# A decoder step's prompt heads and cache rounds: older heads first, query copies on VectorE, a later second gather, and a gate in two parts

## The chip, the cores and the metric

The kernel runs on one core of one Trainium2 chip. The time is the device time of one execution in microseconds (us). The engines of the core are named as in the profile: PE is TensorE with its weight load PEld, DVE is VectorE, ACT is ScalarE, POOL is GpSimd, SP is SyncE, which here only starts DMAs.

## The reference

One inference step of a decoder trunk of two layers, with 256 prompt tokens and 8 samples of 8 tokens each (320 tokens in all). Each layer adds to x the merged output of three branches, each with a sigmoid gate:

```
xn = RMSNorm(x);  (h_pool, ..., h_gate) = split(xn @ w_in)
y_a = pool_mixer(h_pool) * silu(z_pool)
y_b = MLA(h_q, h_kv, h_kr, cache) * silu(z_mla)     # 8 heads, 64 nope + 32 rope, latent 256
y_c = gated_delta(h_qkv, ...) * silu(z_dn)
gates = sigmoid(h_gate)                             # 3 x 1024 columns
x = x + (g0*(y_a@w_br_pool) + g1*(y_b@w_br_mla) + g2*(y_c@w_br_dn)) @ w_out
```

The change lies in the attention of MLA and in the gates that are computed beside it. The prompt attends causally to itself; a sample attends to the 2048 cached tokens of its own 16 pages, which a page table names, and to its own 8 new tokens. Softmax is over both together.

## The kernel before

Every projection is a float32 matmul done as three products: `split_w` makes of a weight block its rounded high part wh (ACT, L196) and the rest wl (a subtraction, L197, on DVE, or on POOL where the call says `spare`), and `mm3` (L209 to 222) sums wh times the high part of xn, wh times its low part, and wl times its high part. A gate is one block of 128 of the 3072 gate columns: `gate_w` loads and splits its weight, `gate_mm` issues 24 matmuls of 128x320 (8 blocks of k, three products each), `gate_out` multiplies by the norm's factor on DVE (L460), takes tanh on ACT (L461) and, if the gate is to be spilled, starts its store from ACT's queue (L464). Gates are spread over the attention, so that PE has work where the attention's chain leaves it without.

From L1332 on the order on PE, DVE, ACT and POOL is the order in which the program is written (a manual schedule); each engine works through its instructions in that order, and waits where an operand isn't ready. There are two parts.

**The heads** (L1349 and on, h from 0 to 10) are the prompt's attention, a pipeline over 8 heads. A step h copies the query of head h into one of two buffers qx (`head_query`: two copies, nope and rope, L1260 and L1261, on POOL), computes its scores (psc on PE, L1272), adds the causal mask while it leaves PSUM (pS on DVE, L1274), takes the two negated maxima (L1276, L1277) and the two exponentials (ACT, L1278 and L1279). Then it scales head h-1 (reciprocal on DVE L1283, 128 columns on ACT L1284, 256 columns on POOL L1285), transposes the P of head h-2 (pT on PE, L1290, copied by ACT, L1292), and multiplies head h-3's P with the values (po, L1299 and L1300), which DVE puts into zs (L1301). `gather(bb)` starts two indirect DMAs on POOL's queue, kv (2 MB, L1133) and kr (256 KB, L1134), for the pages of sample bb; gather 0 stands ahead of the heads, gather 1 behind head 0's scores. Two gates (steps `GP`) lie in the heads, and five DVE transposes (`flip`, L1153 and L1150) turn sample 0's gathered keys into KT and krT in steps 4 to 8.

**The rounds** (L1376 and on, bb from 0 to 7) are the samples' attention to the cache. A round scales the scores sc (L1163) into S with a running maximum (`soften`, L1185), joins it with the maximum over the sample's own tokens (mo) and across the two halves of the partitions (`swap`, L1180: two copies of 64 partitions), takes exp (L1195 to L1197), transposes P (PT on PE, L1212, copied by ACT in two parts, L1213; PTn for the own tokens, L1221), multiplies it with kv (pv, 33 matmuls, L1235 and L1239), scales the result (o, L1241) and computes the next round's sc. Beside it run one or two gates (GL), and the DVE transposes of the next sample's keys, five a round. `weigh` (L1199) makes the factor 1/sum for o. Three kv buffers and two kr buffers hold the gathers; q is loaded by four DMAs of SP's queue (L1140), the gate weights by others of it into four buffers.

Of the kernel before, what the change touches and what calls it, by code (L numbers as in the profile page):

```python
# [11 lines left out]
F32 = mybir.dt.float32  # L12
# [30 lines left out]

GP, GL, SPILL = (0, 4), (2, 2, 2, 2, 2, 2, 1, 1), 14

# [71 lines left out]
def trunk(tc, I, O, layers=2):  # L117
# [90 lines left out]

    def mm3(out, w, x, nk, first=0):  # L209
        wh, wl = w  # L210
        xh, xl = x
        if l == 0 and turn[0] <= WLP:
            for k in range(nk):
                nc.tensor.matmul(out, wh[:, k, :], xh[:, first + k, :], start=k == 0, stop=False)
                nc.tensor.matmul(out, wh[:, k, :], xl[:, first + k, :], start=False, stop=False)
            for k in range(nk):
                nc.tensor.matmul(out, wl[:, k, :], xh[:, first + k, :], start=False, stop=k == nk - 1)
            return
        for k in range(nk):
            nc.tensor.matmul(out, wh[:, k, :], xh[:, first + k, :], start=k == 0, stop=False)  # L220
            nc.tensor.matmul(out, wh[:, k, :], xl[:, first + k, :], start=False, stop=False)  # L221
            nc.tensor.matmul(out, wl[:, k, :], xh[:, first + k, :], start=False, stop=k == nk - 1)  # L222
# [187 lines left out]
    for l in range(layers):  # L410
# [40 lines left out]

        def gate_mm(tag, w):
            b = ps(tag, "gate")
            mm3(b[:, :T], w, xn, 8)
            return b
# [429 lines left out]
        so = p2.tile([128, 4, 64], F32, name="so")  # L885
        mo = p2.tile([128, 4], F32, name="mo")
        cko = p2.tile([64, 256], F32, name="cko")
# [72 lines left out]
        def latent_queries():  # L960
# [22 lines left out]
            for j in range(4):  # L983
# [4 lines left out]
                stt(so[:, j], sc[:, :64], SCALE, c("win")[:, 48 - 16 * j : 112 - 16 * j], mult, add)  # L988
            nc.vector.tensor_reduce(mo, so, AX.X, amax)

# [178 lines left out]
        def stats(bb):  # L1169
            mx = pa.tile([128, 12], F32, tag="mx", name="mx", bufs=2)  # L1170
            nc.gpsimd.memset(mx, 0.0)
            nc.gpsimd.memset(mx[:, 2:3], NEG)
            own, j = halves[bb % 2], bb // 2
            nc.gpsimd.tensor_copy(mx[own, 2:3], mo[own, j : j + 1])
            return mx

        def swap(eng, mx, k):

            for er, other in (halves, halves[::-1]):
                eng.tensor_copy(mx[er, 11:12], mx[other, k : k + 1])  # L1180

        def soften(bb, sc, mx):
# [5 lines left out]
            )  # L1188
            tt(mx[:, 3:4], mx[:, 1:2], mx[:, 2:3], amax)  # L1189
            swap(nc.gpsimd, mx, 3)  # L1190
            return S
# [6 lines left out]

        def weigh(mx):  # L1199

            tt(mx[:, 9:10], mx[:, 5:6], mx[:, 6:7], add)
            swap(nc.vector, mx, 9)
            tt(mx[:, 10:11], mx[:, 9:10], mx[:, 11:12], add)
            nc.vector.reciprocal(mx[:, 10:11], mx[:, 10:11])
# [52 lines left out]
        def head_query(h):  # L1257
            p, er = eight[h]
            e, rr = h % 2, slice(32 * (h % 4), 32 * (h % 4) + 32)
            nc.gpsimd.tensor_copy(qx[e][er], qn[er, p, :TP])  # L1260
            nc.gpsimd.tensor_copy(qx[e][rot[e]], qr[rr, h // 4, :TP])  # L1261

# [19 lines left out]
        def head_scale(S, st2):  # L1282
            nc.vector.reciprocal(st2[:, 4:6], st2[:, 2:4])  # L1283
            act(S[:, :128], S[:, :128], AF.Copy, scale=st2[:, 4:5])  # L1284
            nc.gpsimd.tensor_scalar(S[:, 128:], S[:, 128:], st2[:, 5:6], None, mult)  # L1285
# [45 lines left out]
        with tc.manual_schedule(engines={mybir.EngineType.PE, mybir.EngineType.DVE, mybir.EngineType.Activation, mybir.EngineType.Pool}):  # L1331
# [6 lines left out]
            q4 = load_q(0)  # L1338
            nm, w = gate_w()
            for t in range(2):  # L1340
# [8 lines left out]
            for h in range(11):  # L1349
                if h < 8:  # L1350
                    head_query(h)
                    hs[h] = head_scores(h)
                if h == 0:
                    gather(1)
                if h - 1 in hs:
                    head_scale(*hs[h - 1])
                if h - 2 in hs:
                    hp[h - 2] = head_turned(hs[h - 2][0])
                if h - 3 in hs:
                    head_attend(h - 3, hp[h - 3])  # L1360
                if h in GP:
                    b = gate_mm("A", w)
                    gate_out(nm, b, True)
                    if h == GP[-1]:
                        pair[0] = paired[0] = 1
                    nm, w = gate_w() if h < GP[-1] else (None, None)
                if 4 <= h < 9:
                    flip(0, keys, parts_[h - 4])
            phc.close()
# [6 lines left out]
            for bb in range(NB):  # L1376
                more = bb + 1 < NB
                S = soften(bb, sc, mx)
                if bb + 2 < NB:
                    gather(bb + 2)  # L1380
                if more:
# [11 lines left out]
                if more:  # L1393
                    flip(bb + 1, keys, 4)
                    flip(bb + 1, keys, 2)
                for nm, w in gs[1:]:
                    b = gate_mm("A", w)
                    gate_out(nm, b, bb < 6)
                weigh(mx)
                PT = turned_p(S)  # L1400
                PTn = turned_own(bb)
                o = attend(bb, PT, PTn, mx)
                if more:
# [118 lines left out]
```

## Time and profile before

| | |
|---|---|
| Median of 3 runs | 1108.27 us (1102.31 to 1115.26) |
| The profiled execution | 1106.15 us, span 1104.4 us |
| Mean granted clock of PE in it | 0.952 |
| Busy | PE 90%, DVE 64%, ACT 42%, POOL 30% |
| Heads of layer 0 (first psc to first sc) | 289.27 to 341.41 us |
| Heads of layer 1 | 827.08 to 877.31 us |
| One round with two gates | 18.1 us |

Busy shares are means over the span, in which the projections with a nearly full PE take most of the time. What the heads and the rounds wait for is read in their own stretches. A clock of 1.00 is PE's upper level of 2.4 GHz, 0.50 the lower of 1.2 GHz. In the timelines, "xN" joins N like instructions, and the bracket at a row's end gives the idle time of that engine before it and what ended that.

### The profile page before, as it was taken

Reading aid. Unit: us, or ns where it says so; the run is one execution under the profiler, and the core shown is the slowest. Engines: PE = TensorE matmul, PEld = TensorE weight load, DVE = VectorE, ACT = ScalarE, POOL = GpSimd, SP = SyncE. Lnnn points to the kernel's source line nnn. Section 1 sums busy time; section 2 is a strip of 40 time slices with the busy share of each in tenths; the row PEclk is TensorE's granted clock in tenths of the full one; section 3 lists DMA queues with packets and bytes.
Section 4 is the critical chain, followed back from the end, with each engine's and each line's share of the span. In section 5 each row is a group of like instructions: output and inputs, shape, how many; then the busy total and the mean of one; then the engine's idle time right before and its main releaser. Section 6 shows DMA issues by size and latency. Waiting matters only on the chain.

```text
span 1104.4 us, 24792 instructions
## 1 busy us (share of the span) xinstructions
PE 996.2 (90%) x10179; PEld 867.7 (79%) x10179; DVE 709.0 (64%) x1341; ACT 460.7 (42%) x826; POOL 336.4 (30%) x527
## 2 busy tenths in 40 slices
PE   8988999999668999989988978999994799999996
PEld 7867898988456878779978867899783577777996
DVE  3999875656336656548748988656752665554872
ACT  5563253633323333244545534345242333333553
POOL 3655221232232111016355542211432211110531
PEclk8999899999868999999999989999996899999998
DMA  8523333625704666348763332364274186741961
GB/s 223 167 77 99 93 102 104 177 76 135 243 21 147 205 237 199 114 132 232 179 192 96 90 87 75 104 175 111 83 211 127 37 260 187 258 149 55 271 189 48
DMA packets 202698, 159.22 MB, mean 144 GB/s; under 512 B 27704, under 2 KB 191826, under 8 KB 200010
## 3 DMA queue, kind: packets, MB, share of 16 engines
q1 hardware_dynamic: 176364, 98.47, 32.8%
q0 software_dynamic: 7424, 48.75, 12.4%
q10 hardware_dynamic: 18798, 10.44, 3.3%
q8 instruction: 80, 1.31, 0.5%
q14 instruction: 32, 0.26, 0.1%
HBM read 144.17 MB, written 13.68 MB: 143 GB/s over the span
## 4 chain that ended last, share of the span: by engine, by line
PE 48%; DMA 15%; DVE 14%; issue 13%; ACT 6%; POOL 4%; ACTq 0%; SPq 0%; POOLq 0%; DVEq 0%
DMA kr<-in_cache_k_rope,idr 12%; PE pj L220 5%; PE pj L222 4%; PE pj L221 4%; DVE cy L505 4%; PE br L220 3%; PE br L221 3%; PE br L222 2%; DVE wl L197 2%; PE wo L220 2%; PE wo L221 2%; PE wo L222 2%; PE psc L1272 2%; PE gate L222 2%; PE gate L220 2%
## 5 line engine op out<-in xcount | busy, mean ns | idle before, releaser
L197 DVE TENSOR_TENSOR wl<-wraw,wh 128x1024 fp32r<-128x1024 f32 (+2 forms) x169 | 195.8, 1167 | 107.3 <-ACT wh L196 106.4
L196 ACT ACTIVATE wh<-wraw 128x1024 fp32r<-128x1024 f32 (+1 forms) x180 | 166.2, 935 | 177.3 <-PE pj L221 90.5
L220 PE MATMUL pj<-xnH,wh 128*128 128x320 f32 (+1 forms) x528 | 173.1, 328 | 16.7 <-DVE V L497 8.9
L222 PE MATMUL pj<-xnH,wl 128*128 128x320 f32 (+1 forms) x528 | 170.4, 323 | 6.7 <-DVE wl L197 6.3
L221 PE MATMUL pj<-xnL,wh 128*128 128x320 f32 (+1 forms) x528 | 168.2, 319 | 0.0
L220 PE MATMUL gate<-xnH,wh 128*128 128x320 f32 x384 | 123.9, 323 | 1.5 <-DVE V L497 1.5
L222 PE MATMUL gate<-xnH,wl 128*128 128x320 f32 x384 | 120.7, 314 | 1.6 <-DVE wl L197 1.3
L220 PEld LDWEIGHTS pj<-xnH,wh 128*128 128x128 f32 (+1 forms) x528 | 101.6, 192 | 24.7 <-ACT wh L196 6.9
L221 PE MATMUL gate<-xnL,wh 128*128 128x320 f32 x384 | 119.6, 312 | 0.0
L222 PEld LDWEIGHTS pj<-xnH,wl 128*128 128x128 f32 (+1 forms) x528 | 101.6, 193 | 11.8 <-DVE wl L197 8.1
L221 PEld LDWEIGHTS pj<-xnL,wh 128*128 128x128 f32 (+1 forms) x528 | 101.7, 193 | 3.2 <-issue 1.8
L220 PEld LDWEIGHTS gate<-xnH,wh 128*128 128x128 f32 x384 | 73.1, 190 | 9.2 <-issue 6.9
L1153 DVE STREAM_TRANSPOSE KT<-kv 128x1024 f32<-128x1024 f32 x64 | 78.5, 1226 | 0.1
L222 PEld LDWEIGHTS gate<-xnH,wl 128*128 128x128 f32 x384 | 73.0, 190 | 3.1 <-DVE wl L197 1.8
L221 PEld LDWEIGHTS gate<-xnL,wh 128*128 128x128 f32 x384 | 73.1, 190 | 1.1 <-issue 0.8
L1235 PE MATMUL pv<-kv,PT 128*64 128x256 f32 x512 | 58.8, 382 | 15.0 <-ACT PT L1213 15.0
L220 PE MATMUL br<-yH,wh 128*128 128x320 f32 x192 | 60.4, 318 | 4.2 <-ACT wh L196 2.2
L1235 PEld LDWEIGHTS pv<-kv,PT 128*64 128x64 f32 x512 | 35.4, 137 | 33.3 <-ACT PT L1213 17.2
L221 PE MATMUL br<-yL,wh 128*128 128x320 f32 x192 | 59.8, 313 | 0.0
L1163 PE MATMUL sc<-KT,q 32*64 32x256 f32 x2048 | 59.3, 377 | 0.0
L222 PE MATMUL br<-yH,wl 128*128 128x320 f32 x192 | 59.3, 312 | 0.0
L1180 POOL COPY mx<-mx 64x1 f32<-64x1 f32 x32 | 5.7, 179 | 167.6 <-DVE mx L1189 166.7
(408 smaller groups left out, 2108.8 us busy)
## 6 DMA issues: line engine op xcount, KB each, us to landing
wraw<-in_w_in SPq DMA_DIRECT2D x114, 512.0 KB
wraw<-in_w_out SPq DMA_DIRECT2D x16, 512.0 KB
q<-q4d SPq DMA_DIRECT2D x64, 72.0 KB
gate<-gt ACTq DMA_DIRECT2D x28, 160.0 KB
gt<-gate POOLq DMA_DIRECT2D x28, 160.0 KB, 3.6
wraw<-in_w_br_pool SPq DMA_DIRECT2D x16, 256.0 KB
wraw<-in_w_br_dn SPq DMA_DIRECT2D x16, 256.0 KB
wraw<-in_w_br_mla SPq DMA_DIRECT2D x16, 256.0 KB
```

The lines of the kernel that those rows point to most:

```text
L196: act(h, raw, AF.Copy)
L197: (nc.gpsimd.tensor_tensor if spare or turn[0] in K["lo"] else tt)(lo, raw, h.bitcast(F32), sub)
L220: nc.tensor.matmul(out, wh[:, k, :], xh[:, first + k, :], start=k == 0, stop=False)
L221: nc.tensor.matmul(out, wh[:, k, :], xl[:, first + k, :], start=False, stop=False)
L222: nc.tensor.matmul(out, wl[:, k, :], xh[:, first + k, :], start=False, stop=k == nk - 1)
L505: stt(y, V[:, j : j + 344], wj(j), y, mult, add)
L1153: nc.vector.transpose(v[:, a], kv[:, a * 1024 : a * 1024 + 1024].rearrange("p (i k c) -> p i k c", i=4, k=8))
L1163: nc.tensor.matmul(sc[64 * hf : 64 * hf + 64, g, :256], q4[r, k, :], krT[r, keys_] if k == 8 else KT[r, k, keys_], start=k == 0, stop=k == 8,)
L1180: eng.tensor_copy(mx[er, 11:12], mx[other, k : k + 1])
L1235: nc.tensor.matmul(pv[64 * hf : 64 * hf + 64, :256], PT[:, n * 128 + 64 * hf : n * 128 + 64 * hf + 64], kv[:, r : r + 256], start=n == 0, ...
L1272: nc.tensor.matmul(o, qx[e][kr, tq], kn[e][kr, p, :nk], start=True, stop=True)
```

## The change

In the heads: a step now scales head h-1 before it computes head h's scores; the query copies are DVE's (L1262, L1263) and stand one head ahead (head 0's ahead of the values, head h+1's in step h); the scale of the 128 columns goes from ACT to POOL (L1286, beside the 256 columns, L1287); the weights of both gates have their wl on POOL; the gates move from steps 0 and 4 to steps 1 and 5, their matmuls ahead of `head_attend`, the rest behind it; gather 1 moves from step 0 to step 3; DVE's transposes of the keys move from steps 4 to 8 to steps 3 to 7.

In the rounds: the first swap is DVE's; mo is kept in a form with the other half at a very low value, so that the copy and memset of `stats` go (its one reduction becomes two of 64 partitions, with one memset for a layer); the sum in `weigh` is POOL's, and gather bb+2 stands behind it instead of behind `soften`; in rounds with two gates the second gate's matmuls are issued in two parts of 12, P's transposes between them, and `gate_out`, `weigh` and pv behind the second part.

```diff
-GP, GL, SPILL = (0, 4), (2, 2, 2, 2, 2, 2, 1, 1), 14
+GP, GL, SPILL = (1, 5), (2, 2, 2, 2, 2, 2, 1, 1), 14
...
-        def gate_mm(tag, w):
-            b = ps(tag, "gate")
-            mm3(b[:, :T], w, xn, 8)
+        def gate_mm(tag, w, b=None, ks=(0, 8)):
+            b = b or ps(tag, "gate")
+            mm3(b[:, :T], w, xn, 8, ks=ks)
             return b
...
-        mo = p2.tile([128, 4], F32, name="mo")
+        mo = p2.tile([128, 4, 2], F32, name="mo")
+        nc.gpsimd.memset(mo, NEG)
...
-            nc.vector.tensor_reduce(mo, so, AX.X, amax)
+
+            for e, er in enumerate(halves):
+                nc.vector.tensor_reduce(mo[er, :, e], so[er], AX.X, amax)
...
             nc.gpsimd.memset(mx, 0.0)
-            nc.gpsimd.memset(mx[:, 2:3], NEG)
-            own, j = halves[bb % 2], bb // 2
-            nc.gpsimd.tensor_copy(mx[own, 2:3], mo[own, j : j + 1])
             return mx
...
-            tt(mx[:, 3:4], mx[:, 1:2], mx[:, 2:3], amax)
-            swap(nc.gpsimd, mx, 3)
+            tt(mx[:, 3:4], mx[:, 1:2], mo[:, bb // 2, bb % 2 : bb % 2 + 1], amax)
+            swap(mx, 3)
...
-        def weigh(mx):
-
-            tt(mx[:, 9:10], mx[:, 5:6], mx[:, 6:7], add)
-            swap(nc.vector, mx, 9)
+        def weigh(bb, mx):
+
+            nc.gpsimd.tensor_tensor(mx[:, 9:10], mx[:, 5:6], mx[:, 6:7], add)
+            if bb + 2 < NB:
+                gather(bb + 2)
+            swap(mx, 9)
...
-            nc.gpsimd.tensor_copy(qx[e][er], qn[er, p, :TP])
-            nc.gpsimd.tensor_copy(qx[e][rot[e]], qr[rr, h // 4, :TP])
+            nc.vector.tensor_copy(qx[e][er], qn[er, p, :TP])
+            nc.vector.tensor_copy(qx[e][rot[e]], qr[rr, h // 4, :TP])
...
-            act(S[:, :128], S[:, :128], AF.Copy, scale=st2[:, 4:5])
+            nc.gpsimd.tensor_scalar(S[:, :128], S[:, :128], st2[:, 4:5], None, mult)
...
-            nm, w = gate_w()
+            nm, w = gate_w(True)
+            head_query(0)
...
             for h in range(11):
-                if h < 8:
-                    head_query(h)
-                    hs[h] = head_scores(h)
-                if h == 0:
-                    gather(1)
                 if h - 1 in hs:
                     head_scale(*hs[h - 1])
+                if h < 7:
+                    head_query(h + 1)
+                if h == 3:
+                    gather(1)
+                if h < 8:
+                    hs[h] = head_scores(h)
                 if h - 2 in hs:
                     hp[h - 2] = head_turned(hs[h - 2][0])
+                if h in GP:
+                    b = gate_mm("A", w)
                 if h - 3 in hs:
                     head_attend(h - 3, hp[h - 3])
                 if h in GP:
-                    b = gate_mm("A", w)
                     gate_out(nm, b, True)
                     if h == GP[-1]:
                         pair[0] = paired[0] = 1
-                    nm, w = gate_w() if h < GP[-1] else (None, None)
-                if 4 <= h < 9:
-                    flip(0, keys, parts_[h - 4])
+                    else:
+                        nm, w = gate_w(True)
+                if 3 <= h < 8:
+                    flip(0, keys, parts_[h - 3])
...
                 S = soften(bb, sc, mx)
-                if bb + 2 < NB:
-                    gather(bb + 2)
...
-                for nm, w in gs[1:]:
-                    b = gate_mm("A", w)
-                    gate_out(nm, b, bb < 6)
-                weigh(mx)
+                two = len(gs) > 1
+                if two:
+                    b = gate_mm("A", gs[1][1], ks=(0, 4))
                 PT = turned_p(S)
                 PTn = turned_own(bb)
+                if two:
+                    gate_mm("A", gs[1][1], b, (4, 8))
+                    gate_out(gs[1][0], b, bb < 6)
+                weigh(bb, mx)
                 o = attend(bb, PT, PTn, mx)
```

The order of the instructions at three places follows. In brackets stand the counters for which an instruction waits; those with DMASW count the transfers of POOL's queue, given in turn, and at this place kv and kr of gather 0 have DMASW5 and DMASW6, those of gather 1 DMASW7 and DMASW0.

POOL at the start of layer 0's heads, before:

```order
L1134 DMA kr<-in_cache_k_rope,idr_2158 128x512 [waits DMASW6_49,DMASW0_49]
L1260 COPY qx_3356<-qn 64x256 [waits DMASW4_49,DMASW3_49]
L1261 COPY qx_3356<-qr 32x256 [waits Pool_49]
L1133 DMA kv<-in_cache_kv_latent,idr_2158 128x4096 [waits DMAHW2_49,DMAHW0_49,DMAHW4_49,DMASW7_49,PE_49]
L1134 DMA kr<-in_cache_k_rope,idr_2158 128x512
L1260 COPY qx_3357<-qn 64x256 [waits DMASW6_49,DMASW7_49,DMASW5_49,DMASW0_49]
L1261 COPY qx_3357<-qr 32x256 [waits Pool_49]
L1285 TENSOR_SCALAR pS<-pS,st_3391 128x256 [waits DVE_49,DMASW2_49,Activation_49,Pool_49]
```

and in the changed kernel:

```order
L1137 DMA kr<-in_cache_k_rope,idr_2158 128x512 [waits DMASW6_49,DMASW0_49]
L197 TENSOR_TENSOR wl<-wraw,wh 128x1024 [waits DMAHW2_49]
L1286 TENSOR_SCALAR pS<-pS,st_3395 128x128 [waits DMASW3_49,DMASW2_49,DVE_49]
L1287 TENSOR_SCALAR pS<-pS,st_3395 128x256 [waits Activation_49]
L197 TENSOR_TENSOR wl<-wraw,wh 128x1024 [waits DMAHW4_49,PE_49,Activation_49]
L1286 TENSOR_SCALAR pS<-pS,st_3410 128x128 [waits DVE_49]
L1287 TENSOR_SCALAR pS<-pS,st_3410 128x256
L1286 TENSOR_SCALAR pS<-pS,st_3460 128x128 [waits DVE_49]
L1287 TENSOR_SCALAR pS<-pS,st_3460 128x256 [waits Activation_49]
L1136 DMA kv<-in_cache_kv_latent,idr_2158 128x4096 [waits DMAHW0_49,DMASW7_49]
```

The copies are gone, the wl of the second head gate stands between the scales of heads 0 and 1, and the second gather behind those of head 2. Of the waits for POOL's own transfers, the first copy's stood for older ones, the second copy's for both gathers.

PE in the heads of layer 0 behind the values, before (psc of heads 0 to 2, the gate's first and last matmul):

```order
L1343 MATMUL vv<-wuv,hkv 128x512 x4
L1272 MATMUL psc<-kn,qx_3356 128x128
L1272 MATMUL psc<-kn,qx_3356 128x256
L220 MATMUL gate<-xnH,wh 128x320
...
L222 MATMUL gate<-xnH,wl 128x320
L1272 MATMUL psc<-kn,qx_3357 128x128
L1272 MATMUL psc<-kn,qx_3357 128x256
L1272 MATMUL psc<-kn,qx_3356 128x128
L1272 MATMUL psc<-kn,qx_3356 128x256
L1290 MATMUL pT<-cst,pS 128x128 x3
```

and in the changed kernel:

```order
L1274 MATMUL psc<-kn,qx_3358 128x128
L1274 MATMUL psc<-kn,qx_3358 128x256
L1274 MATMUL psc<-kn,qx_3359 128x128
L1274 MATMUL psc<-kn,qx_3359 128x256
L220 MATMUL gate<-xnH,wh 128x320
...
L222 MATMUL gate<-xnH,wl 128x320
L1274 MATMUL psc<-kn,qx_3358 128x128
L1274 MATMUL psc<-kn,qx_3358 128x256
L1292 MATMUL pT<-cst,pS 128x128 x3
L1274 MATMUL psc<-kn,qx_3359 128x128
L1274 MATMUL psc<-kn,qx_3359 128x256
L1292 MATMUL pT<-cst,pS 128x128 x3
```

The gate is now behind the scores of heads 0 and 1, and head 0's transposes ahead of head 3's scores.

PE in layer 0's first round, from the second gate's last matmuls on, before:

```order
L220 MATMUL gate<-xnH,wh 128x320
L221 MATMUL gate<-xnL,wh 128x320
L222 MATMUL gate<-xnH,wl 128x320
L1212 MATMUL PT<-cst,S 128x128 x8
L1221 MATMUL PTn<-cst,so 64x64
L1235 MATMUL pv<-kv,PT 64x256 x16
```

and in the changed kernel:

```order
L222 MATMUL gate<-xnH,wl 128x320
L1214 MATMUL PT<-cst,S 128x128 x8
L1223 MATMUL PTn<-cst,so 64x64
L220 MATMUL gate<-xnH,wh 128x320
...
L222 MATMUL gate<-xnH,wl 128x320
L1237 MATMUL pv<-kv,PT 64x256 x16
```

Between PTn and pv stand now 12 matmuls of the gate.

## Rows read from the trace of the kernel before

**Rows 1.** The page's parts 1 and 2: busy time, and granted clock in 40 slices.

```profile
PE 996.2 (90%) x10179; PEld 867.7 (79%) x10179; DVE 709.0 (64%) x1341; ACT 460.7 (42%) x826; POOL 336.4 (30%) x527
...
PEclk8999899999868999999999989999996899999998
```

**Rows 2.** Timeline of PE, heads: start us, us, engine, line, operation, tiles, [idle before].

```profile
289.27 0.82 PE L1272 MATMUL psc<-kn,qx 96*128 96x128 f32 x4
...
327.89 1.65 PE L1272 MATMUL psc<-kn,qx 96*128 96x128 f32 x4 [3.00 <-POOL qx L1261]
...
331.02 0.63 PE L1300 MATMUL po<-pPT,vv 128*64 128x128 f32 x2
...
341.41 3.71 PE L1163 MATMUL sc<-KT,q 32*64 32x256 f32 x128
...
827.08 0.82 PE L1272 MATMUL psc<-kn,qx 96*128 96x128 f32 x4
...
877.31 3.06 PE L1163 MATMUL sc<-KT,q 32*64 32x256 f32 x103
```

**Rows 3.** Waits of PE, heads of layers 0 and 1: us in total, times, longest.

```profile
PE psc L1272 <- POOL qx L1261: 18.1, 6, 6.6
...
PE psc L1272 <- POOL qx L1261: 20.0, 6, 7.6
```

**Rows 4.** Windows: us, busy time (and count) by engine, PEclk, DMA share, GB/s.

```profile
281.00:299.00 18.00, 12.62 (x66) 9.37 (x63) 3.81 (x8) 5.67 (x15) 4.65 (x5) 0.88 1.00 348
299.00:318.00 19.00, 10.57 (x31) 6.94 (x32) 6.46 (x18) 5.79 (x19) 5.82 (x11) 0.50 0.15 42
```

**Rows 5.** Chain of waits, 278 to 400: start us, us, what.

```profile
287.56 11.68 DMA kr<-in_cache_k_rope,idr
299.29 0.40 POOL qx L1260
...
366.96 10.48 DMA kr<-in_cache_k_rope,idr
```

**Rows 6.** Timeline of DVE, heads and rounds of layer 0.

```profile
324.72 0.52 DVE L1274 SCALAR_TENSOR_TENSOR pS<-psc,cst 128x384 f32<-128x384 f32 x1
...
326.19 1.23 DVE L1153 STREAM_TRANSPOSE KT<-kv 128x1024 f32<-128x1024 f32 x1
...
371.50 0.31 DVE L1180 COPY mx<-mx 64x1 f32<-64x1 f32 x2
...
382.89 1.24 DVE L1153 STREAM_TRANSPOSE KT<-kv 128x1024 f32<-128x1024 f32 x1
```

**Rows 7.** Waits of PE, rounds of layer 0 (341 to 466).

```profile
PE pv L1235 <- ACT PT L1213: 6.6, 7, 1.0
```

**Rows 8.** Timeline of PE, rounds with two gates and with one.

```profile
367.12 0.39 PE L220 MATMUL gate<-xnH,wh 128*128 128x320 f32 x1
...
370.71 1.04 PE L1212 MATMUL PT<-cst,S 128*128 128x128 f32 x8
...
372.96 3.67 PE L1235 MATMUL pv<-kv,PT 128*64 128x256 f32 x32 [1.04 <-ACT PT L1213]
...
459.59 3.67 PE L1235 MATMUL pv<-kv,PT 128*64 128x256 f32 x32 [0.42 <-ACT PT L1213]
```

**Rows 9.** Timeline of ACT, first gate in the heads (ACTq: its queue's DMA).

```profile
294.18 0.47 ACT L461 ACTIVATE gt<-gt 128x320 f32<-128x320 f32 x1 [2.10 <-DVE gt L460]
299.10 0.35 ACTq L464 DMA_DIRECT2D gate<-gt  x1
299.50 1.06 ACT L196 ACTIVATE wh<-wraw 128x1024 fp32r<-128x1024 f32 x1 [4.85 <-DMA q<-q4d]
```

**Rows 10.** Groups by line: busy us, mean ns of one, idle before.

```profile
L197 POOL TENSOR_TENSOR wl<-wraw,wh 128x1024 fp32r<-128x1024 f32 x11 | 26.6, 2415 | 14.5 <-ACT wh L196 14.4
```

**Rows 11.** Timeline of POOL, heads of layer 0.

```profile
282.58 1.33 POOL L1261 COPY qx<-qr 32x256 f32<-32x256 f32 x1
...
303.42 0.93 POOL L1285 TENSOR_SCALAR pS<-pS,st 128x256 f32<-128x256 f32 x1 [3.29 <-ACT pS L1278]
```

More of the change, by code (lines that the diff above doesn't have):

```diff
@@ L207, in split_x, with mm3 @@
         return i
-    def mm3(out, w, x, nk, first=0):
+    def mm3(out, w, x, nk, first=0, ks=None):
         wh, wl = w
@@ L218, in mm3 @@
             return
-        for k in range(nk):
+        for k in range(*(ks or (0, nk))):
             nc.tensor.matmul(out, wh[:, k, :], xh[:, first + k, :], start=k == 0, stop=False)
@@ L1171, in stats, with swap @@
             nc.gpsimd.memset(mx, 0.0)
-            nc.gpsimd.memset(mx[:, 2:3], NEG)
-            own, j = halves[bb % 2], bb // 2
-            nc.gpsimd.tensor_copy(mx[own, 2:3], mo[own, j : j + 1])
             return mx
-        def swap(eng, mx, k):
+        def swap(mx, k):
             for er, other in (halves, halves[::-1]):
-                eng.tensor_copy(mx[er, 11:12], mx[other, k : k + 1])
+                nc.vector.tensor_copy(mx[er, 11:12], mx[other, k : k + 1])
         def soften(bb, sc, mx):
```

## The prediction

> **What bounds the kernel now.** I read the page first, then the waits of TensorE in the two stretches that the change touches, then the chain of waits there, and last the single instructions. The page says that TensorE is busy 90% of the span, with two dips of its granted clock [rows 1]. The reader is to see there that the kernel as a whole has only some 108 us of idle TensorE to win, plus what is lost at the lower clock. The dips are the heads. In layer 0 they run from the first psc at 289.27 to the first sc at 341.41, 52.1 us; in layer 1 from 827.08 to 877.31, 50.2 us [rows 2]. In them TensorE waits 18.1 and 20.0 us for POOL's query copies, six times each [rows 3]. Beside the idle time there is a second loss: in 299 to 318 the granted clock is 0.50, which is the 1.2 GHz level, and one head's four psc matmuls take 1.65 us instead of 0.82 [rows 2, 4].
>
> The chain names what POOL waits for: the second gather's kr, issued at 287.56 and under way for 11.68 us, and then POOL's copies [rows 5]. The order of the instructions shows why: head 1's first copy waits by name for the counters of all four gather transfers, the two just issued included. From then on every head repeats a circle: psc, pS and its maxima, exp, POOL's scale, POOL's copies, next psc, one after the other. The chain follows kr in the rounds too (366.96, 10.48 us), but there I do not believe it: it lands at 377.44, and VectorE takes up the new keys first at 382.89, with 5.4 us to spare [rows 5, 6]. What a round loses is elsewhere: pv waits for ScalarE's copies of P's transposes, 6.6 us in seven rounds, of which 0.42 in the one-gate round [rows 7, 8].
>
> **Heads, part by part (layer 0, my own timeline).**
> *Query copies.* Two copies a head leave POOL for VectorE, one head ahead. With them the wait for four gathers goes; no compute instruction on POOL waits for a gather afterwards. VectorE's copies of this shape are not in the trace. Bounds are 0.15 (half of the 0.31 that two copies of 64x1 take there) and 0.40, POOL's own price for the shape [rows 5, 6]; I take 0.3, nearer to the row of the same shape, so 0.6 a head.
> *What is late next.* Psc 0 and psc 1 come together (0.7 each), gate 1 follows from 290.7 to 294.3 (24 matmuls, 3.6 us as in a round, 367.12 to 370.71 [rows 8]), then psc 2, pT 0, psc 3, to about 296.1. pT 1 needs head 1's scales. On POOL these now stand behind the second head gate's wl, as the order shows. That wl needs ScalarE's wh, which stands behind the first gate's tanh and store. Now gate 1 follows psc 0 and ends by the same count at 293.6, and its tanh begins at 294.18; so tanh comes 0.6 behind a gate, at 294.9, and takes 0.47, the store 0.35, wh 1.06 [rows 9]: 296.8. POOL's wl takes 2.4 (2415 ns mean [rows 10]): 299.2. Head 1's two scales: 0.93 for 256 columns [rows 11], and for 128 columns, not in the trace on POOL, between 0.46 (half) and 0.93; I take 0.55, since a row's fixed part is small beside 2.4 us for 1024 columns. So pT 1 is at about 300.8, a wait of 4.7 us: **the 18 us of waits do not vanish, about a quarter comes back as a wait for this wl.**
> *The store itself* waits now until 299.10, held 4.85 us by a load of q [rows 9]. In 281 to 299 the DMA engines are full at 348 GB/s, 6.3 MB [rows 4]. One gather (kv 2 MB, kr 0.25 MB) leaves this window, 4.0 MB remain, which at the same rate are through at about 292.6, before the store's turn. I cost that wait at nothing; if it stays, see the rivals.
> *After that VectorE sets the pace*: pS to the end of zs is 1.47 (324.72 to 326.19), one KT transpose 1.23, two copies 0.6 [rows 6]: 3.3 us a head. From 300.8: pT, ACT's copy, po and zs 2.0, a KT 1.2, four heads 13.2, and the last head's exp, scales, pT, copy, po 5: sc at 322.2. POOL's two scales, 1.5 a head, stay beside it, also with gather 1's 2.2 us, which is needed only at the first round.
> *Clock.* A wait of 3.00 us was followed by psc at the lower level (1.65 at 327.89 [rows 2]); so after one of 4.7 us it will be low again. If all later matmuls of the heads ran low, a head's psc, pT and po would be 3.76 us (327.89 to 331.65 [rows 2]) against VectorE's 3.3, and gate 2 twice as long, 3.6 more; with the short pieces at the start and the end doubled too some +9 us, end at 331. At the upper level throughout +0. Gate 2 is a long unbroken run, in which the clock rose before, so I take +3: 325.2, **36 us of heads: 16.1 us saved in layer 0, 14.2 in layer 1.**
> *wl of both gates on POOL* costs 2.4 instead of 1.2 each; the first has from 282 to 290.7 and is covered, the second is the wait above. *ACT's 128-column scale moved to POOL* is in the scales above.
>
> **Rounds.** In six rounds a layer the second gate's last 12 matmuls (1.8 us, half of 3.6) come between P's transposes and pv. ScalarE's copies, which kept pv 1.04 us [rows 8] behind, end within them. Gain (6.6-0.42)/6=1.03 a round, 6.2 a layer, 12.4 together. VectorE's tail behind the gate gets about 1.2 us later, beside a pv of 3.67 [rows 8]: nothing. The first swap on VectorE: two copies of 0.31 together [rows 6], ahead of a KT; exp has slack in two-gate rounds; in round 6 of each layer up to 0.3 is lost, 0.6 in all. mo's two reductions instead of one: 0.3. The gather goes behind the sum mx9, so behind exp: some 2.5 us later, while its use comes 1.0 earlier. Of 5.4 us slack 1.9 remain: nothing, while kr lands within 12.4 us; the slowest of rows 5 took 11.68, at full DMA engines. Four q loads go ahead of the weights on SP's queue: nothing, four weight buffers hold two rounds.
>
> **Sum.** 16.1+14.2+12.4-0.6-0.3 = 41.8. The profiled execution is 1106.15 us (span 1104.4); that gives 1064.4. The median of the runs is 2.1 above it, so 1066 against the median.
>
> **A rule of the skill.** At 282.58 POOL's copy of 32x256 took 1.33 us, where such a copy takes 0.40, while VectorE was in a wl [rows 5, 11]. The Trainium skill, page "SBUF — State Buffer", section "Who interferes with whom", says that a VectorE copy in SBUF, or a VectorE operation with two SBUF inputs, and a GpSimd operation that reads SBUF exclude one another, the second waiting for the whole first. The row agrees. By that rule the copies moved to VectorE can each wait for a scale on POOL; the sum above has none of it, and rival 3 prices it.
>
> **Rivals.**
> 1. *The clock stays low from pT 1 to the end of the heads*: 331 instead of 325.2 in both layers, +11.6: 1077. For it: 299 to 318 has 0.50 throughout. Against: the gaps there were five, here it is one. Chance 0.13.
> 2. *The store still waits for q until 299.1*: wh 299.5 to 300.6, wl 303.0, pT 1 at 304.6, 3.8 us later in each layer: 1074. Against: 2.25 MB fewer in flight. 0.07.
> 3. *VectorE's copies and POOL's scales exclude each other*: up to 0.93 a head [rows 11], seven heads, two layers, 13 us; half of it likelier: 1072, at most 1079. That the one row agrees speaks for it, that POOL is idle half of each turn against. 0.10.
> 4. *The split gate does nothing* (pv waits as long as now for something else, VectorE's tail or the bank): +12.4, 1079. The order shows pv waiting only for the copies, so 0.05.
> 5. *Slower: the later gather lands too late.* VectorE's first KT of the next keys stands ahead of the maximum that exp needs, so a late kr or kv stops the round. Slack 1.9 us over a landing of 10.5; each microsecond beyond costs 6 rounds in 2 layers, 12 us. From a landing of 15.9 us the whole gain of 41.8 is gone; at 17.5 it is 5.1 times 12 = 61 us, 1127. For it: the new issue time meets the gates' stores and the next weights; against: 11.68 is the longest of rows 5, in a stretch with the DMA engines full [rows 4]. 0.04 for that, and 0.03 for a mild form up to 1100.
>
> **The numbers.** My forecast has 0.58: 1066, with its own range 1056 to 1076, the lower end from the clock at the upper level throughout (-6) and copies at 0.15 (0.15 for 2 copies in 4 heads of 2 layers, -2.4), the upper from copies at 0.41 and scales at 0.93 a head. The range of 8 in 10 is 1055 to 1085 and takes in rivals 1 to 4. A measurement of this kernel tells about 1%, 11 us, from no change. Faster by more: the forecast, rivals 1 to 4 (0.93), less a little of their tails and with a little of the mild fifth: 0.93. Within 1%: 0.04. Slower: 0.03.
>
> **What would show it.** Right: the waits for POOL's copies gone; heads of 34 to 38 us; one wait at pT 1 of 3 to 6 us, released by POOL's scales behind wl; pv's wait near 0 in two-gate rounds, a period of about 17.05 instead of 18.1 us; kr landing before VectorE's first KT. Wrong: a wait for a DMA at that KT, several gaps in the heads with the clock at 0.50, or a store in the heads that still ends at 299.

## The result and the profile after

The changed kernel takes 1064.19 us (median of 4 runs, 1063.22 to 1066.27), 0.9592 of the kernel before, with a 95% interval of 0.9528 to 0.9655. The prediction said 1066, and 1055 to 1085. The span of the profiled execution is 1064.5 us against 1104.4. Where it went, from the times at which the stretches begin in the two traces:

| us | before | after | saved | forecast |
|---|---|---|---|---|
| heads, layer 0 (psc to sc) | 52.1 | 35.6 | 16.5 | 16.1 |
| heads, layer 1 | 50.2 | 35.1 | 15.1 | 14.2 |
| rounds, layer 0 (sc to the first br) | 137.5 | 132.5 | 5.1 | 5.9 |
| rounds, layer 1 | 137.8 | 133.1 | 4.7 | 5.9 |
| all else | 726.7 | 728.3 | -1.6 | -0.3 |

The last row is work that the change hardly touches. Between the rounds of layer 0 and the heads of layer 1 the twelve kernels of the next section took 344.8 to 349.9 us, with the same instructions; so a span says little below some 5 us, and the lengths of heads and rounds are the better measure.

The page's first lines answer to [rows 1]:

```profile
PE 995.7 (94%) x10179; PEld 866.4 (81%) x10179; DVE 725.8 (68%) x1387; ACT 456.5 (43%) x810; POOL 338.0 (32%) x469
...
PEclk8999899999989999999998989999998899999998
```

PE's busy time is almost unchanged, its share is up, and the two dips of the clock are shallow now. The timeline of PE in the heads of both layers, for [rows 2]:

```profile
288.94 1.48 PE L1274 MATMUL psc<-kn,qx 96*128 96x128 f32 x8
...
295.46 0.89 PE L1274 MATMUL psc<-kn,qx 128*128 128x128 f32 x4 [0.54 <-DVE qx L1263]
...
299.65 0.33 PE L1292 MATMUL pT<-cst,pS 128*128 128x128 f32 x1 [3.30 <-POOL pS L1286]
300.55 0.69 PE L1292 MATMUL pT<-cst,pS 128*128 128x128 f32 x2 [0.57 <-POOL pS L1287]
...
302.64 1.65 PE L1274 MATMUL psc<-kn,qx 96*128 96x128 f32 x4
...
324.55 3.71 PE L1166 MATMUL sc<-KT,q 32*64 32x256 f32 x128
...
806.62 1.48 PE L1274 MATMUL psc<-kn,qx 96*128 96x128 f32 x8
...
841.72 4.28 PE L1166 MATMUL sc<-KT,q 32*64 32x256 f32 x128
```

The two psc come together, nothing waits for a copy on POOL, and one long wait is left, 3.30 and 0.57 us at pT of head 1, for POOL's scales (817.31 in layer 1, with 3.33 and 0.42); no other wait of PE in the heads reaches 1 us. What POOL and ACT do ahead of it, in their timelines:

```profile
296.59 2.34 POOL L197 TENSOR_TENSOR wl<-wraw,wh 128x1024 fp32r<-128x1024 f32 x1 [2.97 <-ACT wh L196]
298.91 0.69 POOL L1286 TENSOR_SCALAR pS<-pS,st 128x128 f32<-128x128 f32 x1
299.58 0.92 POOL L1287 TENSOR_SCALAR pS<-pS,st 128x256 f32<-128x256 f32 x1
...
295.00 0.35 ACTq L464 DMA_DIRECT2D gate<-gt  x1
295.45 1.06 ACT L196 ACTIVATE wh<-wraw 128x1024 fp32r<-128x1024 f32 x1 [0.48 <-ACT gt L461]
```

This is the chain that the prediction wrote down, within 0.4 us at each step: store, wh, wl to 298.9 (forecast 299.2), scales to 300.5 (300.8). Only the first part of pT is earlier than written, by 1.2 us. Against [rows 9] the store is not held. In the windows, for [rows 4], the heads of layer 0 have this, before and after (us, busy time and count by engine, granted clock, DMA share, GB/s):

```profile
289.30:341.40 52.10, 32.85 (x137) 23.41 (x135) 20.26 (x47) 16.86 (x53) 13.06 (x25) 0.67 0.25 80
```

```profile
288.90:324.50 35.60, 29.09 (x137) 20.82 (x135) 23.84 (x58) 14.73 (x46) 16.88 (x21) 0.81 0.44 131
```

PE idles 6.5 us instead of 19.2: 12.7 of the 16.5 us. The other 3.8 us are the clock: the same matmuls keep PE busy 3.8 us less at 0.81 than at 0.67. In layer 1 it is 14.0 us of idle time and 1.1 of clock (0.82 instead of 0.76). A round with two gates, for [rows 8], in PE's timeline, and the PT of round 6:

```profile
368.36 1.04 PE L1214 MATMUL PT<-cst,S 128*128 128x128 f32 x8
369.33 0.24 PE L1223 MATMUL PTn<-cst,so 64*64 64x64 f32 x1
369.50 0.42 PE L220 MATMUL gate<-xnH,wh 128*128 128x320 f32 x1
369.75 0.31 PE L221 MATMUL gate<-xnL,wh 128*128 128x320 f32 x1
...
371.46 3.67 PE L1237 MATMUL pv<-kv,PT 128*64 128x256 f32 x32
...
435.95 1.09 PE L1214 MATMUL PT<-cst,S 128*128 128x128 f32 x8 [0.54 <-ACT S L1196]
```

In rounds with two gates pv has no idle time ahead of it any more. From the gate's first matmul behind PTn to the next one it is 0.25 us instead of 0.15: taking the gate up again costs PE 0.1 us. VectorE's first KT of the next keys follows its swap at once, so the later gather is not late:

```profile
381.35 0.31 DVE L1180 COPY mx<-mx 64x1 f32<-64x1 f32 x2
381.69 1.25 DVE L1156 STREAM_TRANSPOSE KT<-kv 128x1024 f32<-128x1024 f32 x1
```

### The profile page after: what moved, and what is told of

It reads as the page before. It is cut to its first block, busy times and chain, and to the rows that moved or that the text cites. A ratio compares the mean times of both kernels' runs of the same rounds, so it can differ in the third digit from the quotient of the medians.

```text
span 1064.5 us, 24733 instructions
## 1 busy us (share of the span) xinstructions
PE 995.7 (94%) x10179; PEld 866.4 (81%) x10179; DVE 725.8 (68%) x1387; ACT 456.5 (43%) x810; POOL 338.0 (32%) x469
## 4 chain that ended last, share of the span: by engine, by line
PE 71%; DVE 15%; ACT 5%; issue 3%; DMA 3%; POOL 1%; ACTq 0%; SPq 0%; DVEq 0%; POOLq 0%
PE sc L1166 6%; PE pv L1237 5%; PE gate L220 5%; PE pj L220 5%; PE pj L222 5%; PE gate L222 4%; PE pj L221 4%; PE gate L221 4%; DVE cy L505 4%; PE br L220 3%; PE br L221 2%; DVE wl L197 2%; PE br L222 2%; PE wo L220 2%; PE wo L222 2%
## 5 line engine op out<-in xcount | busy, mean ns | idle before, releaser
L197 DVE TENSOR_TENSOR wl<-wraw,wh 128x1024 fp32r<-128x1024 f32 (+2 forms) x165 | 187.9, 1147 | 69.2 <-ACT wh L196 68.2
L505 DVE SCALAR_TENSOR_TENSOR cy<-V,prm,cy 128x344 f32<-128x344 f32 x72 | 56.5, 804 | 0.5
L1166 PEld LDWEIGHTS sc<-KT,q 32*64 32x64 f32 x2048 | 45.8, 132 | 12.7 <-issue 6.2
```

The costliest lines, as they stand in the source:

```text
L197: (nc.gpsimd.tensor_tensor if spare or turn[0] in K["lo"] else tt)(lo, raw, h.bitcast(F32), sub)
L505: stt(y, V[:, j : j + 344], wj(j), y, mult, add)
L1166: nc.tensor.matmul(sc[64 * hf : 64 * hf + 64, g, :256], q4[r, k, :], krT[r, keys_] if k == 8 else KT[r, k, keys_], start=k == 0, stop=k == 8,)
```

## The experiments

Lengths in us, from each trace; the ratio is that of the runs to the kernel before, with its interval.

| kernel | heads L0, L1 | span | ratio |
|---|---|---|---|
| heads_only | 35.7, 35.1 | 1074.2 | 0.9716 (0.9650 to 0.9782) |
| no_split | 34.7, 35.2 | 1074.2 | 0.9715 (0.9657 to 0.9773) |
| copies_ahead | 40.4, 36.2 | 1082.3 | 0.9825 (0.9766 to 0.9884) |
| gather_only | 44.6, 46.2 | 1091.4 | 0.9887 (0.9825 to 0.9948) |
| copies_pool | 48.8, 46.8 | 1086.6 | 0.9818 (0.9780 to 0.9856) |
| gather_early | 35.5, 35.1 | 1063.5 | 0.9612 (0.9566 to 0.9659) |
| defer2d | 32.0, 32.0 | 1057.5 | 0.9585 (0.9540 to 0.9629) |
| defer2p | 34.5, 32.8 | 1056.9 | 0.9590 (0.9554 to 0.9625) |
| after_again | 35.5, 35.8 | 1062.9 | 0.9610 (0.9581 to 0.9638) |
| act1 | 31.9, 32.3 | 1056.8 | 0.9582 (0.9552 to 0.9612) |
| act2 | 33.4, 31.9 | 1059.6 | 0.9586 (0.9548 to 0.9625) |
| gate2_halves | 30.7, 31.1 | 1058.5 | 0.9575 (0.9541 to 0.9609) |

**The two halves of the gain.** heads_only has the changed heads and the old rounds. no_split undoes only the gate's division (`gate_out` and `weigh` with it):

```diff
                 two = len(gs) > 1
                 if two:
-                    b = gate_mm("A", gs[1][1], ks=(0, 4))
+                    b = gate_mm("A", gs[1][1])
+                    gate_out(gs[1][0], b, bb < 6)
+                weigh(bb, mx)
                 PT = turned_p(S)
                 PTn = turned_own(bb)
-                if two:
-                    gate_mm("A", gs[1][1], b, (4, 8))
-                    gate_out(gs[1][0], b, bb < 6)
-                weigh(bb, mx)
                 o = attend(bb, PT, PTn, mx)
```

> The changed kernel's heads with the rounds as before (first swap on POOL, gather bb+2 straight behind soften, second gate whole, mo and stats as before). My theory (heads about 31.6 us of the gain, rounds about 10): span about 1075 against 1064.5 for the whole change and 1104.4 before, heads of 35 to 36 us in both layers, round period 18.1 us. Rival (the heads carry it all, the rounds' gain is given back elsewhere): 1065. Rival (heads and rounds need each other, heads alone give half): 1085 or more.

> The changed kernel with the second gate of a round undivided ahead of P's transposes; swap on VectorE, mo in two halves and the later gather stay. My theory (pv's wait for ScalarE's copies is all that a round gained, less 0.1 us for one more change of shape on PE): pv waits about 1.0 us again in 12 rounds, span 1075 to 1076, the same as with the old rounds within 1 us. Rival (the later gather and the swap carry part): 1070 or less. Rival (they cost something that the split hides): 1078 or more.

Both come out as the theory said. The rounds of no_split take 138.4 and 137.9 us, those of heads_only 137.5 and 138.4: the other edits of the rounds (swap, mo, gather) neither save nor cost 1 us. PE's longest waits in no_split show the 1 us per round back:

```profile
PE pv L1237 <- ACT PT L1215: 14.7, 16, 1.0
```

**One edit at a time from the kernel before.** copies_ahead moves only the copies:

```diff
+            head_query(0)
             for h in range(11):
+                if h < 7:
+                    head_query(h + 1)
                 if h < 8:
-                    head_query(h)
                     hs[h] = head_scores(h)
...
-            nc.gpsimd.tensor_copy(qx[e][er], qn[er, p, :TP])
-            nc.gpsimd.tensor_copy(qx[e][rot[e]], qr[rr, h // 4, :TP])
+            nc.vector.tensor_copy(qx[e][er], qn[er, p, :TP])
+            nc.vector.tensor_copy(qx[e][rot[e]], qr[rr, h // 4, :TP])
```

> The kernel before with one edit: the query copies on VectorE, one head ahead. Order of scales, gates (steps 0 and 4), wl on VectorE, gather 1 at step 0 and the rounds stay as before. My theory (the circle over POOL's copies is what costs; the first wait stays in another form, since VectorE's wl of the second head gate, ahead of pS of head 1, waits for ScalarE's wh, which stands behind a store held until q has landed): PE's waits for POOL's copies gone, heads of about 38 to 41 us, span 1080 to 1084. Rival (the order of scales and gates carries most of the gain): heads of 46 us or more, span 1094 or more. Rival (the copies alone give all of it): heads of 36 us, span 1074.

Right, in layer 0 at 40.4 us; in layer 1, which the expectation did not set apart, the copies alone give 36.2, nearly all. The remainder in layer 0 is the store that waits for q. In the chain of waits stands the load of q, and behind it the store starts at 302.89. ACT's row and the wait of PE follow from that:

```profile
287.83 14.98 DMA q<-q4d
...
303.29 1.06 ACT L196 ACTIVATE wh<-wraw 128x1024 fp32r<-128x1024 f32 x1 [5.07 <-DMA q<-q4d]
```

```profile
306.24 1.62 PE L1272 MATMUL psc<-kn,qx 96*128 96x128 f32 x4 [8.40 <-DVE qx L1261]
```

In layer 1 the store is not held (822.58), and the same wait is 3.75 us.

gather_only moves only `gather(1)` from step 0 to step 3.

> The kernel before with one edit: gather 1 at step 3 of the heads instead of step 0. Head 1's copy on POOL then waits for gather 0 alone. My theory (the first wait shrinks from 6.6 to 0 to 2.5 us, q lands sooner so that the store is not held, and the circle of POOL's copies, 5 us a head, stays): heads of about 47 to 48 us, span 1095 to 1098. Rival (the wait for the gather is what sets the heads, and the clock falls because of it): heads of 42 us or less, span 1085 or less. Rival (nothing, another wait takes its place): 1103 to 1105.

It saves 7.6 and 4.0 us of heads, between my two cases: 44.6 was expected to be 47 to 48. Head 1's psc no longer waits, and the store is not held. But a wait of the same length stands one head later (PE's timeline):

```profile
302.62 1.65 PE L1272 MATMUL psc<-kn,qx 96*128 96x128 f32 x4 [6.37 <-POOL qx L1261]
```

The reason is in VectorE's timeline: the reciprocal of head 0, for which POOL's scale and then its copies of head 2 wait, stands behind the second gate's wl and the scores of head 1, the younger head. (The trace names head 1's first exponential, 0.14 us later, as what released the scale; it stands behind the same wl and scores.) That order the change turns round.

```profile
298.15 1.22 DVE L197 TENSOR_TENSOR wl<-wraw,wh 128x1024 fp32r<-128x1024 f32 x1 [2.02 <-ACT wh L196]
299.29 0.55 DVE L1274 SCALAR_TENSOR_TENSOR pS<-psc,cst 128x384 f32<-128x384 f32 x1
...
300.40 0.15 DVE L1283 RECIPROCAL st<-st 128x2 f32<-128x2 f32 x1
```

In layer 0 my size was off by the clock: the window 291.2 to 335.8 has 0.81 where I had counted with that of before, and PE's busy time there is 4.4 us shorter. Layer 1, at 0.74 against 0.76, saves its 4.0 us without that.

**One edit taken back from the changed kernel.** copies_pool puts both query copies on POOL again, still one head ahead (`nc.gpsimd` for `nc.vector` in L1262 and L1263).

> The changed kernel with one edit: the query copies back on POOL, still one head ahead. My theory (the copies' place in POOL's queue is what costs: head 1's wait for gather 0, head 3's stand behind the second gate's wl; afterwards a head has slack, POOL's 2.3 us a head being under VectorE's 3.3): heads of 39 to 42 us in both layers instead of 35 to 36, span 1072 to 1078. Rival (the whole circle over POOL's copies is back): heads of 46 us or more, span 1086 or more. Rival (older heads first is enough, the engine of the copies does not matter): heads of 37 us or less, span 1067 or less.

A miss: 48.8 and 46.8 us, 13 and 12 more than the whole change, the size that the first rival named. I had the copy of head 1 wait for gather 0, and thought the rest had slack. These are three of PE's waits, the two longest among them:

```profile
292.88 1.54 PE L1274 MATMUL psc<-kn,qx 128*128 128x128 f32 x4 [2.12 <-POOL qx L1263]
...
306.42 1.65 PE L1274 MATMUL psc<-kn,qx 128*128 128x128 f32 x4 [6.52 <-POOL qx L1263]
...
319.81 1.65 PE L1274 MATMUL psc<-kn,qx 128*128 128x128 f32 x4 [7.66 <-POOL qx L1263]
```

The third is another wait for a gather. Its copy, on POOL, belongs to head 5 and stands behind gather 1, now in the middle of the heads:

```profile
318.94 0.39 POOL L1262 COPY qx<-qn 64x256 f32<-64x256 f32 x1 [5.42 <-DMA kr<-in_cache_k_rope,idr]
```

The second is head 3's copy behind head 1's scales behind the gate's wl. In gather_only, too, head 5's copy waits for gather 1 at its new place, 1.78 us at 317.66; but there the second gate lies ahead of that head's psc on PE, and PE itself waits only 0.31 us (318.55). So as long as the copies are POOL's, one of them waited for the gather at either place that was tried; what it costs the heads depends on the work that PE has meanwhile. The waits for gathers stand on copies into the second of the two buffers (heads 1 and 5) in both kernels; why on these alone I did not find.

gather_early moves `gather(1)` of the changed kernel back to step 0.

> The changed kernel with one edit: gather 1 at step 0 again. No compute instruction of POOL waits for it. My theory (q's load then lands at about 299 in layer 0 and holds ScalarE's store of the first gate, and with it wh and POOL's wl, as rival 2 of the prediction priced): heads of layer 0 at 38 to 40 us, those of layer 1 at 35 to 37, span 1067 to 1070. Rival (its place does not matter): heads 35 to 36 in both, span 1066 or less.

The rival holds: 35.5 and 35.1 us. The store waits for nothing (ACT's timeline), although two gathers are under way:

```profile
297.67 0.35 ACTq L464 DMA_DIRECT2D gate<-gt  x1
298.12 1.06 ACT L196 ACTIVATE wh<-wraw 128x1024 fp32r<-128x1024 f32 x1 [0.48 <-ACT gt L461]
```

What differs is SP's queue (SPq), before, with SP's longest wait for a DMA there, and in gather_early:

```profile
283.69 0.37 SPq L176 DMA_DIRECT2D wraw<-in_w_in  x1
284.28 14.88 SPq L1140 DMA_DIRECT2D q<-q4d  x8
...
SPq L1140 <- DMA wraw<-in_w_in: 10.6, 1, 10.6
```

```profile
282.94 3.35 SPq L1143 DMA_DIRECT2D q<-q4d  x8
288.31 13.71 SPq L176 DMA_DIRECT2D wraw<-in_w_in  x2
```

A row with xN runs from the first issue to the last. Before, the eight loads of q stand behind a weight's load, beside two gathers: the last of them waits 10.6 us for that weight to land before it is issued, and one of them holds the store until 299.10 [rows 9] (in copies_ahead, with the same order, the load that holds it takes the 14.98 us above). In gather_early all eight are issued over 3.4 us, ahead of the weights and before gather 1 starts. In gather_only they stand behind the weight, gather 1 is away, and the store is not held either. So the store was free with either of the two alone, and the change has both. No run changes the order of q's loads by itself: that this order is what frees the store in gather_early is read from the queues, not tested.

**The wait that the change leaves.** In defer2d the second gate's wh stays where it is, and its wl goes to VectorE behind head 2's maxima; in defer2p it goes to the same step on POOL:

```diff
...
                     else:
-                        nm, w = gate_w(True)
+                        rest = []
+                        nm, w = gate_w(True, rest)      # wh now, wl kept for later
                 if 3 <= h < 8:
                     flip(0, keys, parts_[h - 3])
+                if h == 2:
+                    rest.pop()(nc.vector.tensor_tensor) # defer2p: nc.gpsimd
```

> The changed kernel with one edit: of the second head gate's weight only wh stays at the end of step 1; its wl goes to VectorE at the end of step 2, behind head 2's maxima, so that POOL can scale head 1 at once. My theory (the wait of pT for head 1's scales comes from this wl ahead of them, and the lower clock behind it too): that wait, 3.3 and 0.6 us, is gone, the clock in 299 to 310 higher, heads of 30.5 to 32.5 us, span 1056 to 1060. Rival (the wait only moves to head 2 or to VectorE, which gets 1.2 us more): heads of 34.5 us or more, span 1063 or more.

> As the kernel with the deferred wl on VectorE, but the deferred wl stays on POOL, behind head 1's scales and ahead of head 2's. My theory (POOL's wl of 2.4 us keeps VectorE's next query copies back until it ends, by the 1.6 us row of the changed kernel, and head 2's scales by 1 us): heads 0.5 to 1.5 us longer than with wl on VectorE, 31.5 to 33.5, span 1057 to 1062. Rival (copies and wl do not exclude each other; VectorE is the scarcer engine): as short as with wl on VectorE, or shorter.

defer2d does what the theory says: heads of 32.0 us in both layers. pT of head 1 waits no longer (PE's timeline), and the window of the heads of layer 0 has a clock of 0.95:

```profile
298.22 0.67 PE L1295 MATMUL pT<-cst,pS 128*128 128x128 f32 x3
```

```profile
290.90:322.90 32.00, 25.31 (x137) 18.39 (x135) 24.06 (x59) 14.99 (x46) 14.49 (x20) 0.95 0.44 132
```

defer2p is longer, by 0.8 us in layer 1 as expected and by 2.5 in layer 0, more than expected; that window's clock is 0.82, so part of it is PE's. What the theory named is there, on POOL and on VectorE:

```profile
295.98 2.35 POOL L198 TENSOR_TENSOR wl<-wraw,wh 128x1024 fp32r<-128x1024 f32 x1 [0.16 <-ACT wh L196]
```

```profile
296.88 1.59 DVE L1265 COPY qx<-qn 64x256 f32<-64x256 f32 x1
```

The copy takes 1.59 us and ends 0.14 behind the wl; alone it takes 0.29.

**Further along the same line**, after_again being the changed kernel unaltered on the same chip. act1 is defer2d with the rope copy on ScalarE, act2 with both copies there:

```diff
-            nc.vector.tensor_copy(qx[e][rot[e]], qr[rr, h // 4, :TP])
+            act(qx[e][rot[e]], qr[rr, h // 4, :TP], AF.Copy)
```

> The changed kernel unaltered, as the measure for the two others on the same chip: heads of 35 to 36 us in both layers, span 1062 to 1066.

> The kernel with the deferred wl on VectorE, and the rope copy of each query (32x256) on ScalarE. My theory (VectorE sets the heads' pace, one copy of about 0.33 us a head is 1/10 of it, and ScalarE has room): heads 1.5 to 2.5 us shorter than the 32.0 of the deferred kernel, 29.5 to 30.5, span 3 to 5 us under it, 1053 to 1055. Rival (PE's and POOL's chain is as long as VectorE's): 31.5 or more, span 1057 or more.

> As the one before, with both copies of each query on ScalarE. My theory: VectorE has 0.65 us less a head, but ScalarE's copies now stand ahead of its exponentials and pPT copies (some 0.9 us a head), so half of it comes back: heads of 28.5 to 30.5 us, span 1050 to 1055. Rival (ScalarE becomes what exp and pPT wait for): heads of 31 us or more, longer than with one copy.

No heads are shorter than defer2d's by more than 0.1 us, so the rivals hold, with two reservations: act1's span is 0.2 us under its rival's 1057, and act2's heads are longer than act1's in layer 0 only. VectorE has less to do, and PE waits for ScalarE's copies instead, 2.5 us in act1's heads of layer 0 and 4.1 in act2's (act2's waits of PE there): the copy with the longest wait stands behind the wh of the second gate.

```profile
PE psc L1277 <- ACT qx L1266: 4.1, 3, 2.5
```

gate2_halves is defer2d with the second head gate in two parts:

```diff
-                if h in GP:
+                if h == GP[0]:
                     b = gate_mm("A", w)
+                if h == GP[1]:
+                    b = gate_mm("A", w, ks=(0, 4))
+                if h == GP[1] + 1:
+                    gate_mm("A", w, b, (4, 8))
...
```

> The kernel with the deferred wl on VectorE, and the second head gate in two parts of 12 matmuls, in steps 5 and 6. My theory (what is left of the heads is VectorE's order, in which zs of head 2 and a KT stand behind a po that stands behind the whole gate on PE; VectorE idles 1.6 us there, row of the deferred kernel): that idle time falls to 0.5 or less, heads of 30.5 to 31.5 us instead of 32.0 in both layers, span 1055 to 1057. Rival (the chain of a head, psc to po, sets the pace around the gate, and splitting adds a change of shape and keeps a PSUM bank longer): heads of 31.8 us or more, span 1057 or more.

30.7 and 31.1 us, as expected. VectorE's idle time of 1.62 us ahead of head 2's zs is gone; a new one of 0.93 stands ahead of head 3's zs, behind the gate's second part (defer2d, then gate2_halves with both heads):

```profile
310.46 0.42 DVE L1306 SCALAR_TENSOR_TENSOR zs<-po,zs 64x256 f32<-64x256 f32 x1 [1.62 <-PE po L1305]
```

```profile
308.19 0.41 DVE L1306 SCALAR_TENSOR_TENSOR zs<-po,zs 64x256 f32<-64x256 f32 x1
...
312.66 0.43 DVE L1306 SCALAR_TENSOR_TENSOR zs<-po,zs 64x256 f32<-64x256 f32 x1 [0.93 <-PE po L1305]
```

Its span shows none of this: layer 1's rounds took 134.8 us instead of 132.5, the first of them at a clock of 0.90 (832.1 to 850.0) where defer2d had 1.00.

By runs on one chip, act1 has 1059.55 us (1058.58 to 1063.27) and the changed kernel 1064.17 (1062.44 to 1064.63). The versions with the deferred wl have the shorter heads in every trace, by 2 to 5 us a layer with wl on VectorE and by 1.1 and 2.3 us with it on POOL; of their ratios to the kernel before, the intervals still overlap with that of the changed kernel, so a gain of 0.2 to 0.4% over it is likely, and not settled. All of them beat the kernel before.

## Why the prediction was right, step by step

- **The bound.** Right: the heads, by POOL's copies, and pv in the rounds. copies_ahead shows that the copies' move alone brings 11.7 and 14.0 us of heads, and copies_pool that all other edits of the heads bring 3.4 and 3.5 without it. The rest of what the change does there is worth 4.8 and 1.1 us on top of the copies; the larger part is in layer 0, the layer in which copies_ahead still has its store held.
- **The wait that takes its place.** Right in place and cause; it came to 3.30 and 0.57 us instead of 4.7, as pT's first part starts after the 128-column scale and psc 3 waited 0.54 itself. That scale took 0.69 (0.55 taken, bounds 0.46 and 0.93): with 0.92 for 256 columns some 0.46 us, by estimate from these two rows, do not depend on the columns, which the prediction had called small. defer2d, which removes the wl in front, removes the wait.
- **VectorE's pace** behind that wait is not what the trace shows. In this window of the heads of layer 0, from pT 1 to sc, PE is busy 22.2 of 24.9 us and VectorE 16.2:

```profile
299.60:324.50 24.90, 22.18 (x93) 14.77 (x93) 16.19 (x39) 9.39 (x30) 12.31 (x17) 0.73 0.36 123
```

  VectorE waits 8.1 us there for po (2.07, 2.36, 1.77 and 1.88), PE 2.7 us for all others. So PE, in part at the lower level of the clock, is what the stretch mostly waits for (the prediction priced that level at 3.76 us a head against VectorE's 3.3, but took 3 us in all for it). That it came to 24.9 us where 24.4 were forecast (300.8 to 325.2) is so in part luck. act1 fits this: one copy a head less on VectorE did not shorten the heads.
- **The copies** took 0.26 to 0.42 where no wl ran beside them, 0.3 taken. Rival 3 is there in part: beside POOL's wl they took 1.58 and 2.67 us.

```profile
282.55 2.67 DVE L1262 COPY qx<-qn 64x256 f32<-64x256 f32 x1
...
297.50 1.58 DVE L1262 COPY qx<-qn 64x256 f32<-64x256 f32 x1
```

  The first has time to spare, since the next psc is at 288.94. The second delays head 3's pS to 299.48, but POOL comes to head 3's scales only behind head 2's and gather 1, at 304.46. The rule of the Trainium skill, page "SBUF — State Buffer", section "Who interferes with whom", so agrees with the trace for POOL's long wl: both copies end 0.15 us behind it (285.07 and 298.93). Which of the two starts first does not decide it by these records, since the first copy's begins 0.15 us ahead of the wl's (282.70) and yet is the one that waits. Beside the short scales the rows do not show it: the copy at 292.14 takes 0.42 us and ends at 292.56, ahead of the scale beside it (292.05 to 292.71). Such copies took at most 0.42 us in layer 0's heads, so the 0.93 a head of the rival did not come.
- **The clock.** I took +3 us between 0 and 9. It was low from 300.6 to about 307, as forecast, and high in gate 2; and it was low again from 317.4 to 323.6 (0.50), behind two waits of 0.83 and 0.88 us (315.03 and 317.40), which the prediction did not have. The sum came out 0.4 us under the forecast in layer 0, with a wait 0.8 us shorter. Rival 1, a clock that stays low to the end, did not come about.
- **The store** was rightly costed at nothing, but for half the reason: I gave it to the gather alone, and costed q's new place on SP's queue at nothing. The store was free with either alone (gather_only, gather_early). With the gather left where it was, rival 2 would still not have come.
- **The rounds** are the term that was sized too high: a period of 17.17 us (358.47 to 375.64 for sc) instead of 18.09 saves 0.92, not 1.03, because the gate's resumption costs 0.1; in 12 rounds 1.3 us. Round 6 waits 0.54 for exp instead of 0.16, 0.4 each where 0.3 was taken. Together 9.8 us against 11.8; the 0.5 that is left is within what the same rounds vary by (132.5 and 133.1 here, 133.4 and 132.5 in gather_early).
- **The sum.** 16.5 + 15.1 + 5.1 + 4.7 = 41.4 against 42.1 for these four: the heads were 1.3 us better, the rounds 2.0 worse. The rest of the span took 1.6 us more where 0.3 more was forecast, within what it varies; so 39.9 us were saved between the two profiled executions, against 41.8. That the median, 1064.19, lies under the forecast of 1066 even so is luck: the prediction added 2.1 us for the step from the profiled execution to the median, and after the change the profiled execution, 1066.27, is the slowest of its four. Its own range is also wider below than its terms: 1066 - 6 - 2.4 is 1057.6, not 1056.

## What to carry to other kernels

When an engine's copy waits for a DMA, read from the order which other instruction of its queue would inherit the wait; moving the DMA moved the copy's wait here (gather_only, copies_pool), and moving the copy to another engine ended it. Cost a new wait by writing down the queue in front of it step by step (store, wh, wl, scale): this chain came out to 0.4 us, and it named the next improvement. Put a long operation of a gate behind the short ones of an older head on every queue, and measure stretches rather than spans where the rest of the program varies by more than the edit.

## What the runs showed that I had not expected

A gather's wait came back on POOL's copies at both places that the gather had (5.42 us at 318.94 in copies_pool, 1.78 at 317.66 in gather_only). The last of eight loads of q waited 10.6 us for the landing of a weight's load issued ahead of it, beside two gathers; ahead of the weight all eight were issued in 3.4 us. Behind the wait for wl it was PE, not VectorE, that was busy nearly throughout (22.2 of 24.9 us). And of the gain in the heads of layer 0, 3.8 us of 16.5 is the same work at a higher granted clock (0.81 instead of 0.67).
